# Streaming-encoder block: sums of x from its single-precision rows, norms tied to chunk numbers, another selection credit

## The chip, the cores and the metric

One core of a Trainium2 chip runs the whole kernel in one launch. The metric is device time in microseconds (us); the kernel before took 1354.08 us, the median of three executions (1351.22 to 1354.38). The hardware profiler recorded a further execution of 1351.62 us, and all rows below are from that one.

## The reference

One layer for 512 tokens of width 2048, in single precision:

```
h    = rmsnorm(x, norm_w);  proj = h @ w_in
a_q, a_f, a_i, a_g, c_q, c_kv, k_idx_raw, w_idx_raw, b_g, m_a, m_b = split(proj)
y_a  = gated linear recurrence(a_q, a_f, a_i) -> rmsnorm per head -> * silu(a_g)
cq   = rmsnorm(c_q);  q = cq @ w_uq;  q_idx = cq @ w_qidx          # 512 features
k, v = rmsnorm(c_kv) @ w_ukv;   k_idx = layernorm(k_idx_raw)
score = sum over 16 heads of relu(q_idx . k_idx) * w_idx           # per query and key
top 128 visible keys of each query -> attention over them with a relative bias = y_b
out  = rmsnorm(x + (sigmoid(m_a) * (y_a @ w_pa) + sigmoid(m_b) * (y_b @ w_pb)) @ w_out)
```

## The kernel before

**Products.** Every matrix product is made of three single-pass products of rounded high and low parts: `split` (L90) writes the high part on ScalarE and the low part (source less high part) on VectorE, and `mm3` (L94) issues the three matmuls. So every weight chunk is loaded by SyncE (`load`, L145, two raw buffers), split by ScalarE and VectorE (`prep`, L179, two chunks ahead), and only then used by TensorE.

**The start.** `start` (L289) loads x into tiles `x{t}` of pool `p0`, makes the row norms, transposes x on TensorE, and writes the scaled, transposed rows in single precision into tiles `y{t}{g}` (token block t, feature group g), also of `p0`. From these come the high and low parts `xh`, `xl`, which stay in place. The order of all this is the list `START_ORDER` (L20). The pool `p0` is then given up.

**Units with seven products.** The gate columns and the 512 columns of c_q are computed by `pair_unit` (L1227): a unit has eight chunks of 42 matmuls, and a 2x2 block scheme with seven products in place of eight. It needs four sums of blocks of x for each of eight row pairs k. `pair_early` makes them for seven of these: one VectorE addition of `xh` and `xl` (L1184) gives x back, `pair_sums_of` (L1174) makes four sums of 128x256, and `split` writes high and low parts into the tiles `s{k}` of pool `sums`. `pair_late` makes the eighth during the first unit. A unit ends with `evac` (L1255): one ScalarE copy (L1257) and seven VectorE instructions (L1258 to L1264) free its seven PSUM banks, for which the next unit's products wait; its stores go through ScalarE functions (L1268) and SyncE one and two pumps later, out of the tiles `c0` to `c3`.

**The pump.** After each chunk (or part of a job) `pump` (L224) issues loads, the stores that were put off, and then one step of the first generator of each lane (`hgrn`, `top`, `att`, `norm`, `misc`, `t5`, in this order). A generator gives way with `yield`; a step that has nothing to do is a bare `yield`. All engines take their instructions in the order in which they were issued here.

**Norms.** In the lane `norm`, during the gate units: `kidx_gen` (L618) normalises k_idx, `q_squares` (L542) sums the squares of c_q, which it loads from a scratch tensor into `c0` and `c1`, and `q_rows` (L576) loads c_q once more and scales and splits it. Their places are set by counts of bare `yield`s. Sums over the partitions are a matmul with ones (`row_sums`, L570); Ln and Exp on ScalarE (`rstd_row`, L536) make the root.

**Selection.** `top_gen` (L681) finds the 128 largest scores of each query, 48 rounds of `V.max` and `V.match_replace` (L695, L696) over 256, 384 and 512 keys. It runs beside the recurrence (`hgrn_gen`, L782), which sets `R.load` at each of its steps, and beside `norm_gen` (L592), the norm of c_kv. How many rounds a pump issues is set by a credit:

```
while credit <= 0:
    yield
    credit += 2.9 - R.load - bool(lanes["norm"])      # L692
credit -= 0.4 + 0.27 * (b + 1)                        # 0.94, 1.21, 1.48 for b = 1, 2, 3
```

**Behind the selection.** Job `uq_job(0)` leaves its two PSUM banks held (L1366); `open_att` (L1334) finishes the recurrence generators that are still due (gated output L963, L964, its split into `hy`, L969), then evacuates the two held banks (`uq_evac`, L983 on ScalarE and L984 on VectorE), and `ukv_job(0)` (L987) needs these banks for its second half.

Of the kernel before, what the change touches and what calls it, by code (L numbers as in the profile page):

```python
# [44 lines left out]
F32 = mybir.dt.float32  # L45
FR = mybir.dt.float32r
AF = mybir.ActivationFunctionType
OP = mybir.AluOpType
# [13 lines left out]
STILL, MOVED, RANK = 16, 48, 16  # L62

EVEN = 0
EARLY = 7
MO = (0, 128, 384, 768)


# [1 line left out]
def hybrid_block(ctx, tc, x, norm_w, w_in, lb_table, gnorm_a, q_norm_w, kv_norm_w, w_uq,  # L70
# [19 lines left out]
    def split(hi, lo, src):  # L90
        A.activation(hi, src, AF.Copy)  # L91
        V.tensor_tensor(lo, src, hi.bitcast(F32), op=OP.subtract)  # L92
# [37 lines left out]
    def enter(name, side=None, space=None):  # L130
        cm = tc.tile_pool(name=name, bufs=1, side=side, reuse_waits="tile")
        pools[name] = (cm, cm.__enter__())
        return pools[name][1]
# [1 line left out]
    def leave(name):  # L135
        pools.pop(name)[0].__exit__(None, None, None)

    R = SimpleNamespace(load=0.0)


    specs = []
# [146 lines left out]

    def start():  # L289
        R.v0 = enter("v0")  # L290
        p0 = enter("p0", side="right")
        ident = p0.tile([128, 128], F32, name="ident")
        A.dma_start(ident, c_ident)
        HF = D // 2
        nw = p0.tile([16, 128], F32, name="nw")
        wc = p0.tile([128, 16], F32, name="wc")
        xs = [[p0.tile([128, HF], F32, name=f"x{t}{i}") for i in range(2)] for t in range(4)]
        ys = [[p0.tile([128, 4, 128], F32, name=f"y{t}{g}") for g in range(4)] for t in range(4)]
        sq = p0.tile([128, HF], mybir.dt.bfloat16, name="sq")
        st = p0.tile([128, 4, 4], F32, name="st")  # L300
        rows = p0.tile([128, 128], F32, name="rows")
# [45 lines left out]
            return slice(t * 128, t * 128 + 128)  # L347

        def y_of(t, g):
            return ys[t][g]  # L350

        def factor(t, i):
            return st[:, t, i:i + 1]
# [58 lines left out]
                V.tensor_copy(widx[:, t, :], accs[t][:, 256:272])  # L412

        def dg(t):
            spreads[t] = diag, p0.tile([128, 128], F32, name=f"rrow{t}"), None
            V.tensor_scalar(spreads[t][0], ident, factor(t, 3), None, op0=OP.mult)

        def sp(t):
# [120 lines left out]
        A.activation(r, r, AF.Exp, scale=-0.5)  # L539
        return r  # L540

    def q_squares():  # L542
        for j0 in (0, 2):
            for _ in range(3):
                yield
            ts = [R.g.tile([128, 2, 256], F32, name=f"c{i}").rearrange("p a b -> p (a b)") for i in range(2)]
            for i, t in enumerate(ts):
                SP.dma_start(t, cq_d[j0 + i])
            yield
            yield  # L550
            for t in ts:
                A.activation(t, t, AF.Square)
            if j0 == 0:
                V.tensor_add(R.rq, *ts)
            else:
                V.tensor_add(ts[0], *ts)
                V.tensor_add(R.rq, R.rq, ts[0])
            for _ in range(3):
                yield
        sh, sl = R.cqh[:, 3, :], R.cql[:, 3, :]  # L560
        split(sh, sl, R.rq)
        yield
        ps = row_sums(sh, sl)
        for _ in range(2):
            yield
        rstd_row(ps, 512, R.rq)
        for _ in range(5):
            yield

    def row_sums(sh, sl):  # L570
        ps = bank("ns")
        mm(ps, ones_r, sh, True, False)
        mm(ps, ones_r, sl, False, True)
        return ps

    def q_rows():  # L576
        for j0 in (0, 2):
            for _ in range(3):
                yield
            ts = [R.g.tile([128, 2, 256], F32, name=f"c{i}").rearrange("p a b -> p (a b)") for i in range(2)]  # L580
            for i, t in enumerate(ts):
                SP.dma_start(t, cq_d[j0 + i])
            yield
            for i, t in enumerate(ts):
                V.scalar_tensor_tensor(t, t, c_qw[:, j0 + i:j0 + i + 1], R.rq, op0=OP.mult, op1=OP.mult)
                A.activation(R.cqh[:, j0 + i, :], t, AF.Copy)
                yield
                V.tensor_tensor(R.cql[:, j0 + i, :], t, R.cqh[:, j0 + i, :].bitcast(F32), op=OP.subtract)
            yield
            yield  # L590

    def norm_gen(raw, n, w, hi, lo):  # L592
        ss = []
# [16 lines left out]
        for j in range(n):  # L610
# [3 lines left out]
            yield  # L614
            V.tensor_tensor(lo[:, j, :], t, hi[:, j, :].bitcast(F32), op=OP.subtract)
            yield

    def kidx_gen():  # L618
        t, parts = R.rq, (R.cqh[:, 2, :], R.cql[:, 2, :])
        SP.dma_start(t, kx_d)  # L620
        for _ in range(3):
            yield
        split(*parts, t)
        yield
        ps = row_sums(*parts)
        for _ in range(2):
            yield
        V.scalar_tensor_tensor(t, ps, -1.0 / 128, t, op0=OP.mult, op1=OP.add)
        for _ in range(4):
            yield  # L630
        s = R.g.tile([128, 2, 256], F32, name="c3").rearrange("p a b -> p (a b)")
        A.activation(s, t, AF.Square)
        split(*parts, s)
        yield
        ps = row_sums(*parts)
        for _ in range(2):
            yield
        rstd_row(ps, 128, s)
        yield
        V.scalar_tensor_tensor(t, t, c_iw, s, op0=OP.mult, op1=OP.mult)  # L640
        V.tensor_scalar(t, t, c_ib, None, op0=OP.add)
        split(R.kih, R.kil, t)
        yield
        yield


    IDX_SCALE = 16 ** -0.5 * 128 ** -0.5

# [32 lines left out]
    def top_gen():  # L681

        credit = 0.0
        V.memset(R.M[:, 0:128], 0.0)
        for b in range(4):
            V.memset(R.M[0:64, MO[b] + b * 128 + 64:MO[b] + b * 128 + 128], NEG)
        for b in (1, 2, 3):
            m = R.M[:, MO[b]:MO[b] + b * 128 + 128]
            for i in range(16):
                while credit <= 0:  # L690
                    yield
                    credit += 2.9 - R.load - bool(lanes["norm"])  # L692
                credit -= 0.4 + 0.27 * (b + 1)
                m8 = R.s.tile([128, 8], F32, name="m8", bufs=2)
                V.max(m8, m)  # L695
                V.match_replace(m, m8, m, GONE)  # L696
                if i == 15:
                    V.tensor_scalar(m, m, -2e38, NEG, op0=OP.is_gt, op1=OP.mult)
# [438 lines left out]
    def open_norms():  # L1137
        R.c = enter("ranks", side="right")
        R.cqh = R.c.tile([128, 4, T], FR, name="cqh")
        R.cql = R.c.tile([128, 4, T], FR, name="cql")  # L1140
        R.r = enter("raws", side="right")
        R.kih = R.r.tile([128, T], FR, name="kih")
        R.kil = R.r.tile([128, T], FR, name="kil")
        R.rq = R.r.tile([128, T], F32, name="rq")
        R.i = enter("norms", side="right")
        R.x = enter("sums")

    def open_pairs():
        drain("norm")
# [18 lines left out]
            xs.append(cut + [a[:, 768:1024] if b is None else b])  # L1168
        return parts

    def pair_rows(k):
        return (x[k // 2][:, 2 * (k % 2):2 * (k % 2) + 2, :].bitcast(F32) for x in (xh, xl))

    def pair_sums_of(a, d):  # L1174
        a11, a21, a12, a22 = a
        V.tensor_tensor(d[0], a21, a22, op=OP.subtract)
        V.tensor_tensor(d[2], a11, a21, op=OP.subtract)
        V.tensor_tensor(d[1], d[0], a11, op=OP.subtract)
        V.tensor_tensor(d[3], d[1], a12, op=OP.add)

    def pair_early():
        for k in range(EARLY):
            a = R.i.tile([128, 2, T], F32, name="xa", bufs=2)
            V.tensor_tensor(a, *pair_rows(k), op=OP.add)  # L1184
            d = R.i.tile([128, 4, 256], F32, name="sv", bufs=2)
            pair_sums_of([a[:, i, j:j + 256] for i in (0, 1) for j in (0, 256)], [d[:, i, :] for i in range(4)])
            yield
            hi, hi4, lo, lo4 = sums_place(k)
            df = d.rearrange("p q n -> p (q n)")
            split(hi, lo, df[:, 0:768] if hi4 is not None else df)  # L1190
            if hi4 is not None:
                split(hi4, lo4, df[:, 768:])
            yield

    def pair_late():
        for k in range(EARLY, 8):
            ae, ao, da, db = (R.g.tile([128, 2, 256], F32, name=f"c{i}") for i in range(4))
            for i, a in enumerate((ae, ao)):
                V.tensor_tensor(a.rearrange("p a b -> p (a b)"), *(x[:, i, :] for x in pair_rows(k)), op=OP.add)
            pair_sums_of([a[:, j, :] for a in (ae, ao) for j in (0, 1)], [t[:, j, :] for t in (da, db) for j in (0, 1)])  # L1200
            yield
            hi, _, lo, _ = sums_place(k)
            for i, d in enumerate((da, db)):
                n = slice(i * 512, i * 512 + 512)
                split(hi[:, n], lo[:, n], d.rearrange("p a b -> p (a b)"))

    def x_pair(k):

# [18 lines left out]
    def pair_unit(at, n, rhs, evac, tokens_out=False, ahead={}):  # L1227
# [3 lines left out]
        for k in range(n):  # L1231
# [8 lines left out]
                    mm3(p[:, f, :], *ops, k == 0 and f == 0, k == n - 1)  # L1240
            if k == n - 1:
                evac(ps)
            pump()
            if k in ahead:
                ahead[k]()
# [49 lines left out]
    c_rhs = lambda k: (R.cqh[:, k, :], R.cql[:, k, :])  # L1295

    lane("misc", lb_gen)
    lane("misc", pair_early)
    feat_job(w_in, 4608, 2, NK, 4, x_rhs, ckv_evac)
    feat_job(w_in, 4864, 1, NK, 4, x_rhs, kx_evac)  # L1300
    ai_job(1, early=True)
    lane("misc", pair_late)
    pair_job(w_in, [4096, 4352], NK // 2, x_pair, pair_evac([cq_d[0:2], cq_d[2:4]], [None, None]))
    for gen in (kidx_gen, q_squares, q_rows):
        lane("norm", gen)
# [401 lines left out]
```

## Time and profile before

| | |
|---|---|
| median of three executions | 1354.08 us |
| profiled execution, whole | 1351.62 us |
| its span in the profile | 1349.8 us |
| TensorE matmul busy | 1327.1 us (98%) |
| TensorE weight load busy | 1244.6 us (92%) |
| VectorE busy | 1110.1 us (82%) |
| ScalarE busy | 698.7 us (52%) |
| GpSimd busy | 54.1 us (4%) |
| HBM read, written | 168.09 MB, 36.45 MB |

Busy time is the sum of an engine's instructions; what the span holds beyond it is idle time of that engine. The profiled execution is 1.8 us longer than its span: that is what lies around the program.

### The profile page before, as it was taken

The numbers are of one execution on the slowest core, as the hardware profiler recorded it, in microseconds if no ns is written. First come the engines' busy times: TensorE is split into PE (matmuls) and PEld (weight loads), VectorE is DVE, ScalarE is ACT, GpSimd is POOL, SyncE is SP. The second block draws the span as 40 slices with busy tenths as digits, with TensorE's granted clock in tenths as the row PEclk, the third lists the DMA queues.
The fourth block names the chain that finished last, engine by engine and source line by source line (L and its number), as shares of the span: only waits on it lengthen the run. The fifth ranks groups of instructions, "written<-read, shape, count | busy, mean of one in ns | idle before, by whom it ended". The sixth has DMA issues, their size and how long they took to land.

```text
span 1349.8 us, 27460 instructions
## 1 busy us (share of the span) xinstructions
PE 1327.1 (98%) x11202; PEld 1244.6 (92%) x11202; DVE 1110.1 (82%) x1805; ACT 698.7 (52%) x1129; POOL 54.1 (4%) x63
## 2 busy tenths in 40 slices
PE   8999999999999999999999999899999999999997
PEld 8889999999999999999999888788888888899996
DVE  7988888988889888886787989885656658899997
ACT  8444456555555444443765566546534334454454
POOL 0000000000000000000000000020101100001112
PEclk9999999999999999999999999999999999999999
DMA  6253444534544444444524324254856556654533
GB/s 225 58 167 113 149 138 128 161 122 141 172 146 152 141 141 141 115 136 143 191 70 142 111 80 126 90 171 153 287 164 204 199 172 218 209 181 144 201 141 126
DMA packets 143089, 204.76 MB, mean 152 GB/s; under 512 B 10689, under 2 KB 80882, under 8 KB 142834
## 3 DMA queue, kind: packets, MB, share of 16 engines
q1 hardware_dynamic: 142674, 202.74, 47.4%
q8 instruction: 88, 1.44, 0.4%
q14 instruction: 39, 0.32, 0.1%
q10 hardware_dynamic: 288, 0.26, 0.1%
HBM read 168.09 MB, written 36.45 MB: 152 GB/s over the span
## 4 chain that ended last, share of the span: by engine, by line
PE 91%; DVE 5%; ACT 2%; DMA 1%; issue 1%; SPq 0%; DVEq 0%; ACTq 0%
PE pp L95 16%; PE pp L97 16%; PE pp L96 16%; PE acc L95 11%; PE acc L97 11%; PE acc L96 11%; PE hl L100 1%; PE ho L100 1%; PE acc L100 1%; DVE xl L390 1%; PE sc L95 1%; PE sc L96 1%; PE sc L97 1%; DMA fr<-in_w_in_dram 0%; DVE wl L92 0%
## 5 line engine op out<-in xcount | busy, mean ns | idle before, releaser
L174 ACT ACTIVATE wh<-sv 128x512 fp32r<-128x512 f32 x280 | 169.2, 626 | 132.8 <-DVE sv L167 90.4
L172 ACT ACTIVATE bh<-wr 128x768 fp32r<-128x768 f32 x140 | 118.2, 844 | 183.7 <-PE pp L96 75.5
L95 PE MATMUL pp<-s,wh 128*128 128x256 f32 x672 | 185.8, 276 | 1.9 <-DVE c L1262 1.9
L96 PE MATMUL pp<-s,wh 128*128 128x256 f32 x672 | 185.5, 276 | 0.0
L97 PE MATMUL pp<-s,wl 128*128 128x256 f32 x672 | 185.5, 276 | 0.0
L176 DVE TENSOR_TENSOR wl<-sv,wh 128x1024 fp32r<-128x1024 f32 x140 | 171.0, 1221 | 4.9
L175 DVE TENSOR_TENSOR bl<-wr,bh 128x768 fp32r<-128x768 f32 x140 | 133.6, 954 | 43.8 <-ACT bh L172 43.8
L95 PEld LDWEIGHTS pp<-s,wh 128*128 128x128 f32 x672 | 126.1, 188 | 2.2 <-issue 2.2
L97 PEld LDWEIGHTS pp<-s,wl 128*128 128x128 f32 x672 | 126.2, 188 | 0.0
L96 PEld LDWEIGHTS pp<-s,wh 128*128 128x128 f32 x672 | 126.2, 188 | 0.0
L95 PE MATMUL pp<-xh,bh 128*128 128x256 f32 x448 | 123.8, 276 | 0.7 <-ACT c L1257 0.7
L97 PE MATMUL pp<-xh,bl 128*128 128x256 f32 x448 | 123.7, 276 | 0.0
L96 PE MATMUL pp<-xl,bh 128*128 128x256 f32 x448 | 123.7, 276 | 0.0
L167 DVE TENSOR_TENSOR sv<-wr 128x512 f32<-128x512 f32 x140 | 98.2, 702 | 4.2 <-DMA wr<-in_w_in_dram 2.5
L95 PE MATMUL acc<-yh,wh 128*128 128x512 f32 x256 | 100.2, 391 | 0.0
L92 DVE TENSOR_TENSOR wl<-wr,wh 128x1024 fp32r<-128x1024 f32 (+1 forms) x66 | 79.4, 1202 | 25.1 <-ACT wh L91 24.9
L97 PE MATMUL acc<-yh,wl 128*128 128x512 f32 x256 | 99.8, 390 | 0.0
L96 PE MATMUL acc<-yl,wh 128*128 128x512 f32 x256 | 99.7, 390 | 0.0
L91 ACT ACTIVATE wh<-wr 128x1024 fp32r<-128x1024 f32 (+1 forms) x66 | 68.1, 1032 | 61.1 <-PE acc L96 36.2
L95 PE MATMUL acc<-xh,wh 128*128 128x512 f32 x240 | 96.2, 401 | 0.0
L97 PE MATMUL acc<-xh,wl 128*128 128x512 f32 x240 | 93.9, 391 | 1.2 <-DVE wl L92 1.2
L96 PE MATMUL acc<-xl,wh 128*128 128x512 f32 x240 | 93.5, 390 | 0.0
(405 smaller groups left out, 3799.4 us busy)
## 6 DMA issues: line engine op xcount, KB each, us to landing
wr<-in_w_in_dram SPq DMA_DIRECT2D x136, 512.0 KB, 3.7
wr<-in_w_out_dram SPq DMA_DIRECT2D x28, 512.0 KB, 3.8
mg<-gate_d SPq DMA_DIRECT2D x48, 256.0 KB, 3.5
gate_d<-c SPq DMA_DIRECT2D x44, 256.0 KB, 4.9
wr<-in_w_in_dram SPq DMA_DIRECT2D x36, 256.0 KB, 2.9
wr<-in_w_pa_dram SPq DMA_DIRECT2D x16, 512.0 KB, 4.0
wr<-in_w_pb_dram SPq DMA_DIRECT2D x16, 512.0 KB, 4.1
wr<-in_w_qidx_dram SPq DMA_DIRECT2D x8, 512.0 KB, 3.3
```

Of the source, the lines that this page charges most:

```text
L91: A.activation(hi, src, AF.Copy)
L92: V.tensor_tensor(lo, src, hi.bitcast(F32), op=OP.subtract)
L95: PE.matmul(ps, lh, rh, start=first, stop=False, skip_group_check=True)
L96: PE.matmul(ps, lh, rl, start=False, stop=False, skip_group_check=True)
L97: PE.matmul(ps, ll, rh, start=False, stop=last, skip_group_check=True)
L100: PE.matmul(ps, l, r, start=first, stop=last, skip_group_check=True)
L167: V.tensor_tensor(sv[:, 0:2, :], b[:, 1:3, :], b[:, 0:1, :].to_broadcast([128, 2, 256]), op=OP.add)
L172: A.activation(bh, b[:, 1:4, :], AF.Copy)
L174: A.activation(vh[:, i:i + 2, :], sv[:, i:i + 2, :], AF.Copy)
L175: V.tensor_tensor(bl, b[:, 1:4, :], bh.bitcast(F32), op=OP.subtract)
L176: V.tensor_tensor(vl, sv, vh.bitcast(F32), op=OP.subtract)
L390: V.tensor_tensor(xl[g][:, :, tokens(t)], y_of(t, g), xh[g][:, :, tokens(t)].bitcast(F32), op=OP.subtract)
```

## The change

Three things. First, x and y are tiles of the pool `sums` and stay: y is one tile per feature group, `[128, 2048]`, and `pair_gen` makes the sums straight from it, two row pairs at a time (four instructions of 128x512 each), for all eight; `pair_early`, `pair_late` and the addition of `xh` and `xl` go. The sums of the first four row pairs are written over the tiles of x, those of the last four over the tiles of y. Second, the norm generators wait for chunk numbers (`chunk(2)`: go on in a pump after chunk 2 of a unit); `q_squares` loads c_q once, into the places of `cqh`, and `q_rows` reads it there. Third, the credit of the selection loses 0.3 in place of 1 while the lane `norm` is not empty.

```diff
-EARLY = 7
-    R = SimpleNamespace(load=0.0)
+    R = SimpleNamespace(load=0.0, chunk=0)
 def start():
+        R.x = enter("sums")
-        nw = p0.tile([16, 128], F32, name="nw")
+        nw = p0.tile([128, 128], F32, name="nw")[0:16, :]
-        xs = [[p0.tile([128, HF], F32, name=f"x{t}{i}") for i in range(2)] for t in range(4)]
-        ys = [[p0.tile([128, 4, 128], F32, name=f"y{t}{g}") for g in range(4)] for t in range(4)]
+        xs = [R.x.tile([128, 2048 + 64 * (t == EVEN)], F32, name=f"x{t}", tag=f"s{t}") for t in range(4)]
+        xs = [[x[:, 0:HF], x[:, HF:D]] for x in xs]
+        R.ys = [R.x.tile([128, 2048], F32, name=f"y{g}", tag=f"s{4 + g}").rearrange(
+            "p (t j n) -> p t j n", t=4, j=4) for g in range(4)]
...
+    def chunk(*ks):
+        yield
+        while R.chunk not in ks:
+            yield
+    def spare(i):
+        return R.g.tile([128, 2, 256], F32, name=f"c{i}").rearrange("p a b -> p (a b)")
+    def q_squares():
+        raw = [R.cqh[:, j, :].bitcast(F32) for j in range(4)]
+        for j in range(4):
+            SP.dma_start(raw[j], cq_d[j])
+        for j in (0, 2):
+            yield from chunk(2 + j // 2)
+            s = [spare(j), spare(j + 1)]
+            for i in range(2):
+                A.activation(s[i], raw[j + i], AF.Square)
...
+        yield from chunk(0)
+        split(R.cql[:, 0, :], R.cql[:, 1, :], R.rq)
+        yield
+        ps = row_sums(R.cql[:, 0, :], R.cql[:, 1, :])
+        for _ in range(2):
+            yield
+        rstd_row(ps, 512, R.rq)
+    def kidx_gen():
...
+        yield from chunk(2)
+        split(*parts, t)
+        yield
+        ps = row_sums(*parts)
+        yield
+        yield from chunk(0)
+        V.scalar_tensor_tensor(t, ps, -1.0 / 128, t, op0=OP.mult, op1=OP.add)
+        yield from chunk(2)
+        s = spare(3)
+        A.activation(s, t, AF.Square)
+        split(*parts, s)
+        yield
+        ps = row_sums(*parts)
+        yield
+        yield from chunk(0)
+        A.activation(ps, ps, AF.Ln, bias=eps, scale=1.0 / 128)
+        A.activation(ps, ps, AF.Exp, scale=-0.5)
+        yield from chunk(1)
+        V.scalar_tensor_tensor(t, t, c_iw, ps, op0=OP.mult, op1=OP.mult)
+        V.tensor_scalar(t, t, c_ib, None, op0=OP.add)
+        yield from chunk(2)
+        split(R.kih, R.kil, t)
+        yield
     def q_rows():
...
+        for j in range(4):
+            yield from chunk(2)
+            t = spare(0)
+            V.scalar_tensor_tensor(t, R.cqh[:, j, :].bitcast(F32), c_qw[:, j:j + 1], R.rq, op0=OP.mult, op1=OP.mult)
+            A.activation(R.cqh[:, j, :], t, AF.Copy)
+            yield from chunk(3)
+            V.tensor_tensor(R.cql[:, j, :], t, R.cqh[:, j, :].bitcast(F32), op=OP.subtract)
+        yield
 def top_gen():
-                    credit += 2.9 - R.load - bool(lanes["norm"])
+                    credit += 2.9 - R.load - 0.3 * bool(lanes["norm"])
-    def pair_early():
...
-    def pair_late():
...
+    def pair_gen():
+        for g, y in enumerate(R.ys):
+            d = R.i.tile([128, 2, 4, 256], F32, name="sv", bufs=2)
+            a11, a21, a12, a22 = (y[:, t:t + 2].rearrange("p t (k i) n -> p t k i n", i=2)[:, :, :, i, :]
+                                  for i in (0, 1) for t in (0, 2))
+            q = [d[:, :, i, :].rearrange("p k (t n) -> p t k n", t=2) for i in range(4)]
+            V.tensor_tensor(q[0], a21, a22, op=OP.subtract)
+            V.tensor_tensor(q[2], a11, a21, op=OP.subtract)
+            V.tensor_tensor(q[1], q[0], a11, op=OP.subtract)
+            V.tensor_tensor(q[3], q[1], a12, op=OP.add)
+            yield
+            for i in range(2):
+                hi, hi4, lo, lo4 = sums_place(2 * g + i)
+                df = d[:, i].rearrange("p q n -> p (q n)")
+                split(hi, lo, df[:, 0:768] if hi4 is not None else df)
+                if hi4 is not None:
+                    split(hi4, lo4, df[:, 768:])
+                yield
 def pair_unit(...):
+            R.chunk = k
             pump()
-    lane("misc", pair_early)
+    lane("misc", pair_gen)
-    lane("misc", pair_late)
```

## Rows read from the trace of the kernel before

**Rows 1.** The page: the span, and busy time, share of the span and instructions of each engine.

```profile
span 1349.8 us, 27460 instructions
PE 1327.1 (98%) x11202; PEld 1244.6 (92%) x11202; DVE 1110.1 (82%) x1805; ACT 698.7 (52%) x1129; POOL 54.1 (4%) x63
```

**Rows 2.** What TensorE waited for in the whole span: the waiting line, the releaser, us in total, times, the longest.

```profile
PE acc L95 <- DVE aq L984: 5.4, 1, 5.4
PE pp L95 <- DVE c L1262: 1.9, 2, 1.1
PE pt L377 <- DMA x<-in_x_dram: 1.6, 1, 1.6
...
PE acc L97 <- DVE wl L92: 1.2, 1, 1.2
PE acc L96 <- DVE wl L92: 0.9, 1, 0.9
...
PE pp L95 <- ACT c L1257: 0.7, 1, 0.7
```

**Rows 3.** The timeline of TensorE, only matmuls ahead of which it was idle (start, duration, instruction, idle time and what ended it).

```profile
70.63 0.50 PE L97 MATMUL acc<-xh,wl 128*128 128x512 f32 x1 [1.21 <-DVE wl L92]
...
77.24 0.39 PE L96 MATMUL acc<-wl,xh 128*128 128x256 f32 x1 [0.88 <-DVE wl L92]
...
215.36 0.39 PE L95 MATMUL pp<-xh,bh 128*128 128x256 f32 x1 [0.70 <-ACT c L1257]
...
219.63 0.36 PE L95 MATMUL pp<-s,wh 128*128 128x256 f32 x1 [1.11 <-DVE c L1262]
...
411.75 0.36 PE L95 MATMUL pp<-s,wh 128*128 128x256 f32 x1 [0.76 <-DVE c L1262]
...
877.65 0.58 PE L95 MATMUL acc<-wh,ckh 128*128 128x256 f32 x1 [5.41 <-DVE aq L984]
```

**Rows 4.** VectorE's groups of instructions between 50 and 112 us, by line and shape: count, busy us and mean ns of one, idle time before them.

```profile
L1184 DVE TENSOR_TENSOR xa<-xh,xl 128x1024 f32<-128x1024 f32 x7 | 8.5, 1219 | 0.0
...
L167 DVE TENSOR_TENSOR sv<-wr 128x512 f32<-128x512 f32 x5 | 3.4, 685 | 0.0
L1179 DVE TENSOR_TENSOR sv<-sv,xa 128x256 f32<-128x256 f32 x7 | 3.0, 425 | 0.2
```

**Rows 5.** The timeline of VectorE around the two waits at 70 and 77 us, and then one row of ScalarE.

```profile
67.16 1.22 DVE L1184 TENSOR_TENSOR xa<-xh,xl 128x1024 f32<-128x1024 f32 x1
...
69.89 0.68 DVE L92 TENSOR_TENSOR wl<-wr,wh 128x512 fp32r<-128x512 f32 x1
...
75.96 1.23 DVE L92 TENSOR_TENSOR wl<-wr,wh 128x1024 fp32r<-128x1024 f32 x1 [0.31 <-ACT wh L91]
...
74.87 1.06 ACT L91 ACTIVATE wh<-wr 128x1024 fp32r<-128x1024 f32 x1 [3.28 <-DMA wr<-in_w_in_dram]
```

**Rows 6.** The timeline of VectorE, and then of ScalarE, in the gate units between 180 and 220 us.

```profile
209.98 0.74 DVE L640 SCALAR_TENSOR_TENSOR rq<-rq,cols,c 128x512 f32<-128x512 f32 x1
...
211.94 0.69 DVE L92 TENSOR_TENSOR kil<-rq,kih 128x512 fp32r<-128x512 f32 x1 [0.70 <-ACT kih L91]
...
216.08 0.68 DVE L1258 TENSOR_TENSOR c<-pp,c 128x512 f32<-128x512 f32 x1
...
218.80 0.68 DVE L1262 TENSOR_TENSOR c<-pp,c 128x512 f32<-128x512 f32 x1
...
181.75 2.19 ACT L1268 ACTIVATE c<-c 128x512 f32<-128x512 f32 x4
...
191.81 0.63 ACT L632 ACTIVATE c<-rq 128x512 f32<-128x512 f32 x1 [2.63 <-DMA gate_d<-c]
...
205.09 1.28 ACT L539 ACT_TABLE_LOAD   x1
...
214.73 0.58 ACT L1257 ACTIVATE c<-pp 128x512 f32<-128x512 f32 x1
```

**Rows 7.** The timeline of VectorE from 869 us on: the last two rounds of the selection, and what follows them.

```profile
869.38 0.69 DVE L695 MAX8 m<-M 128x8 f32<-128x512 f32 x1
...
870.89 0.69 DVE L695 MAX8 m<-M 128x8 f32<-128x512 f32 x1
...
872.75 0.74 DVE L963 SCALAR_TENSOR_TENSOR hk<-ho,cols,hk 128x512 f32<-128x512 f32 x1
...
875.52 1.47 DVE L92 TENSOR_TENSOR hy<-hk,hy 128x512 fp32r<-128x512 f32 x2
876.91 1.28 DVE L984 SCALAR_TENSOR_TENSOR aq<-acc,aq 128x512 fp32r<-128x512 f32 x2
```

**Rows 8.** The timeline of ScalarE in the same stretch: the last of the four instructions that `L963` needs.

```profile
868.91 1.06 ACT L958 ACTIVATE hk<-hk 128x1024 f32<-128x1024 f32 x1
```

**Rows 9.** Two stretches of 5 us: start:end, length, then busy us and instructions of PE, PEld, DVE, ACT and POOL, the granted TensorE clock, DMA share and GB/s; below them the matmul with which the next job begins.

```profile
875.00:880.00 5.00, 2.35 (x11) 2.35 (x12) 4.88 (x8) 3.63 (x6) 0.00 (x0) 0.52 0.57 211
880.00:885.00 5.00, 5.00 (x26) 4.59 (x26) 2.98 (x5) 2.14 (x3) 0.00 (x0) 0.80 0.86 289
...
882.52 0.40 PE L95 MATMUL acc<-xh,wh 128*128 128x512 f32 x1
```

**Rows 10.** The timeline of VectorE in the recurrence beside which rounds are moved: the first instruction after a score product, and the first half of a round over 256 keys.

```profile
721.11 0.69 DVE L834 TENSOR_TENSOR hq<-hq,tot 128x512 f32<-128x512 f32 x1 [0.74 <-PE hl L100]
...
730.26 0.42 DVE L695 MAX8 m<-M 128x8 f32<-128x256 f32 x1
```

More of the change, by code (lines that the diff above doesn't have):

```diff
@@ L349, in y_of @@
         def y_of(t, g):
-            return ys[t][g]
+            return R.ys[g][:, t]
         def factor(t, i):
@@ L414, in dg @@
         def dg(t):
-            spreads[t] = diag, p0.tile([128, 128], F32, name=f"rrow{t}"), None
+            spreads[t] = diag, p0.tile([128, 128], F32, name=f"rrow{t}", tag=("rrow", "nw")[t]), None
             V.tensor_scalar(spreads[t][0], ident, factor(t, 3), None, op0=OP.mult)
@@ L540, in rstd_row @@
         return r
[L542 to L548, printed above, removed]
-            yield
[L550 to L568, printed above, removed]
+    def chunk(*ks):
+        yield
+        while R.chunk not in ks:
+            yield
+    def spare(i):
+        return R.g.tile([128, 2, 256], F32, name=f"c{i}").rearrange("p a b -> p (a b)")
     def row_sums(sh, sl):
@@ L574, in row_sums @@
         return ps
-    def q_rows():
[L577 to L590, printed above, removed]
+    def q_squares():
[7 more added lines that the diff above has]
+                A.activation(s[i], raw[j + i], AF.Square)
+            if j == 0:
+                V.tensor_add(R.rq, *s)
+            else:
+                V.tensor_add(s[0], *s)
+                V.tensor_add(R.rq, R.rq, s[0])
+        yield from chunk(0)
[5 more added lines that the diff above has]
+        rstd_row(ps, 512, R.rq)
@@ new lines, in kidx_gen @@
+    def kidx_gen():
+        t, parts = R.rq, (R.cqh[:, 2, :], R.cql[:, 2, :])
+        SP.dma_start(t, kx_d)
+        yield
[22 more added lines that the diff above has]
+        yield
@@ L616, in norm_gen @@
             yield
[L618 to L644, printed above, removed]
     IDX_SCALE = 16 ** -0.5 * 128 ** -0.5
@@ L1145, in open_norms @@
         R.i = enter("norms", side="right")
-        R.x = enter("sums")
     def open_pairs():
@@ L1169, in sums_place @@
         return parts
[L1171 to L1179, printed above, removed]
-    def pair_early():
[L1182 to L1186, printed above, removed]
-            yield
[L1188 to L1193, printed above, removed]
@@ L1195, in pair_late @@
-    def pair_late():
[L1196 to L1205, printed above, removed]
+    def pair_gen():
[8 more added lines that the diff above has]
+            V.tensor_tensor(q[3], q[1], a12, op=OP.add)
+            yield
+            for i in range(2):
[5 more added lines that the diff above has]
+                yield
```

## The prediction

> **What bounds the kernel now.** I read the page's busy times first: TensorE's matmuls fill 1327.1 of 1349.8 us [rows 1], so everything that is not TensorE idle time or a lower TensorE clock can give back nothing, and VectorE's 82% matter only where TensorE waits for it. The change takes no matmul away. So the most that it can bring is in the list of TensorE's waits [rows 2], and the second view, TensorE's timeline, says where they lie [rows 3]: two early ones on low parts of weights (70.63 and 77.24 us: 1.21 + 0.88 = 2.09), three at the head of a unit, on its predecessor's evacuation (215.36, 219.63, 411.75: 0.70 + 1.11 + 0.76 = 2.57), and one of 5.41 ahead of 877.65, on the evacuation of the held banks behind the selection. These three places are just those that the three parts of the change touch. Third, the table of stretches: after the long wait the granted clock is 0.52 of full speed in 875 to 880 us and 0.80 in 880 to 885 [rows 9], that is, TensorE works at its lower level (1.2 GHz) for a while. Before that it had stood still for those 5.41 us. With 2.35 us of work in the first stretch and 5 in the second this cost about 2.35 x 0.48 + 5 x 0.20 = 2.1 us.
>
> **Part A, sums of x.** It removes seven additions of 1.22 us, and 28 instructions of 0.42 become part of 16 of 128x512, each some 0.69 by another instruction of that shape [rows 4]: 20 us of VectorE for seven row pairs become 11 for eight. The splits stay. The eighth pair's work leaves the first unit, where TensorE did not wait for it: worth nothing there. At 70 us VectorE is behind TensorE: it had just added x [rows 5], and the low part that TensorE wanted at 70.63 - 1.21 = 69.4 came at 69.89 + 0.68 = 70.6. Up to there the lane had made four sums and three splits, 4 x 2.9 = 11.6 us without the splits. The new one is at its third step of sums, 3 x 4 x 0.69 = 8.3, and at one more split, about 1.2: 2.1 us less, more than the 1.2 that are missing. The second wait hangs on a load that ScalarE waited for [rows 5]; SyncE can issue it when the first low part has freed the raw buffer, so it too comes about 2 us sooner, and the low part ends near 75.1, with TensorE wanting it near 75.2: covered, but barely. Bounds 1.2 (the load does not follow) to 2.09; I take **2.0**.
>
> What is late next: the same loads. What is added: four-dimensional operands on the sums; I price them as plain ones, and the cover at this place is VectorE's new slack. The shared tiles (x in one tile per token block, y in one per feature group) cost something only if a transpose were to wait for the other half of x, one more wait like the 1.61 us on x [rows 2]; I take 0, since `xh` was such a shared tile already and was written and read by regions. Bounds 0 and 1.6.
>
> **Part B, norms by chunk.** Ahead of 215.36 the end of `kidx_gen` ran in the last chunks of a unit: two table loads of 1.28 us each, the last products at 209.98, the split at 211.94 [rows 6]. So ScalarE's evacuation copy came at 214.73, VectorE's share of it began at 216.08 and reached L1262, for which TensorE waited, at 218.80 [rows 6]. In the new order nothing of a norm is left for chunks 4 to 7, and the lateness must be made up by then. I take the 411.75 wait, on the same line, for the same thing with `q_rows`. Moved with the steps: Ln and Exp of `kidx_gen` now queue on ScalarE in the first pump of a unit behind the 2.19 us of stores [rows 6], with about 4 us of their own; the split of the coming chunk waits behind them, VectorE behind that, and TensorE has two prepared chunks as cover. `spare(0)` makes VectorE wait, in four units, for a store to land, as ScalarE did for 2.63 us in the unit before 215 [rows 6]; TensorE waited for nothing behind that until 215.36 [rows 3], so I price these at 0, with the lost cover as a lateness of 2.6 us at chunk 2 that five chunks have to absorb. The c_q loads on SyncE's queue fall from eight to four, issued in one pump, in front of a weight load that lies two chunks ahead: 0. The three waits are worth 2.57 if all go and 0 if new lateness takes their place; one leftover of half a microsecond in a crowded unit (squares, or Ln and Exp) seems fair: **2.1**.
>
> **Part C, the credit.** By the code the lane `norm` is full for eight additions to the credit, so 8 x 0.7 = 5.6 more is credited, 3.8 rounds at the last price of 1.48. I followed the credit pump by pump with the loads that the recurrence sets: the last round is issued two pumps earlier, and the last two pumps, which had two rounds each, have none. The rounds are 870.89 - 869.38 = 1.51 us apart, and the gated output L963 stood behind them until 872.75 [rows 7]. The other thing that L963 needs, the Exp, ended at 868.91 + 1.06 = 869.97 [rows 8]. So of 6 us of rounds taken away only 872.75 - 870.03 = **2.72** reach TensorE: the next lateness is ScalarE's Ln and Exp, bound to TensorE's own products, then L963, L964, `hy` and the evacuation, the same chain of 877.65 - 872.75 = 4.9 us as before [rows 3, 7]. The wait shrinks from 5.41 to 2.69 and does not go. Bounds 0 to 5.41.
>
> Then the clock. A pause of 1.61 us [rows 2] was followed by nothing of the kind, one of 5.41 by the lower level. 2.69 lies between, nearer to the first; I take the full clock, **2.1** more, with ends 0 and 2.1.
>
> The rounds moved forward lie beside the recurrence. The worst new neighbour is ahead of 721.11: two more rounds over 256 keys, about 0.9 each by the half round of 0.42, against an idle time of 0.74 [rows 10]; one us of lateness runs into the next step, whose score product I see losing **0.1**. Bounds 0 and 1.1.
>
> **Sum.** 2.0 + 2.1 + 2.72 + 2.1 - 0.1 = 8.8 us. Against the profiled execution that gives 1351.62 - 8.8 = 1342.8. The executions known lie in two pairs, 1351.22 and 1351.62, 1354.08 and 1354.38; the profiled one is 2.5 below the median shown. I take the middle of the four, 1352.85, and forecast **1344.0**.
>
> **The rivals.** *The clock falls all the same.* The new pause of 2.69 us is longer than any that this trace shows without a fall, so the granted clock may read as in 875 to 885 once more [rows 9]: 2.1 us are not won, 1346.1. The Trainium skill, TensorE: Matmul & The Clock Gate, section on the HAM clock gate, speaks for it: the monitor's window runs freely, so one and the same pause can cost the clock in one execution and not in the next; this trace has one fall only and cannot show that. Chance 0.12.
>
> *The early parts do not do what they say.* The low parts at 70 and 77 us wait for loads rather than for VectorE, and the heads of units find other lateness (VectorE behind a store). For it: the ScalarE row that waits 3.28 us for a load [rows 5] and the 2.63 [rows 6]; against it: the releasers named are VectorE's [rows 2]. Only part C is left, 4.8 us: 1348.0. Chance 0.12.
>
> *Slower: the moved rounds hold up the recurrence.* VectorE takes its work in order; a round that sits between a score product and the next decay holds the following score product. By my count five pumps get an extra round there. It decides where a round exceeds VectorE's idle time, 0.74 at 721.11 [rows 10]. At up to 1.51 each that is 7.5 us, and the gated output is then as late as it was, so part C gives nothing: 1352.85 - 4.1 + 7.5 = 1356.3. Against it: rounds that come earlier are also rounds that are missing later, so VectorE catches up. Chance 0.06.
>
> *Nothing shows*: all is given back in small waits, 1351 to 1354. Chance 0.05. The forecast itself has 0.65.
>
> **How the numbers follow.** The low end is the fastest time shown less everything, 1351.22 - (2.09 + 2.57 + 5.41 + 2.1) = 1339; the high end takes in the rival with part C alone and two us of scatter. Range 1339.5 to 1350. A measurement of this kernel tells about 0.3% (4 us) from no change, so faster means below 1350. That holds nearly all of the forecast (0.63 of 0.65), most of the clock's rival (0.10) and under half of the third (0.05): 0.78. Slower (above 1358) is part of the recurrence's rival and of what I have not thought of: 0.06. The rest, 0.16, is the same.
>
> **What would show it.** Right: no wait on a low part near 70 to 77 us; none at the heads of the units at 215 and 411; a wait on L984 of 2 to 3.5 us with the granted clock at 1.00 behind it; L963 straight behind the Exp, not behind a round. Wrong: that wait at 5 us again, or none at all (then I have mistaken what L963 waits for); a clock under 0.9 after it; waits of score products on VectorE between 700 and 860 us; an evacuation that begins late in the units with squares or with Ln and Exp; a start longer by over a microsecond.

## The result and the profile after

The changed kernel takes 1345.38 us (median of four executions, 1344.59 to 1346.9) against 1353.26 for the kernel before on the same chip: a ratio of 0.9945, 95% interval 0.9928 to 0.9962. Five further executions in another session gave 1346.65 against 1352.32, a ratio of 0.9957 (0.9945 to 0.997); the median of all nine is 1345.67. The forecast of 1344.0 was 1.4 to 1.7 us too low. The profiled execution took 1345.36 us with a span of 1343.5. All rows below come from it unless another kernel is named. Of all executions behind this document one, of the kernel of experiment 11, took 2699.77 us, about twice the others; no profile shows why, and its ratio leaves it out.

First the page: the span and TensorE's busy time, which fell by 1.0 only [rows 1].

```profile
span 1343.5 us, 27423 instructions
PE 1326.1 (99%) x11202; PEld 1243.8 (93%) x11202; DVE 1095.7 (82%) x1779; ACT 700.7 (52%) x1128; POOL 53.7 (4%) x63
```

What TensorE waited for (line, releaser, us in total, times, longest); it answers to [rows 2]. L981 is the line that was L984, L1242 that was L1262, L91 that was L92.

```profile
PE acc L94 <- DVE aq L981: 2.7, 1, 2.7
PE pp L94 <- DVE c L1242: 1.9, 2, 1.0
...
PE acc L95 <- DVE wl L91: 0.7, 1, 0.7
PE acc L96 <- issue: 0.7, 1, 0.7
```

TensorE's timeline, matmuls with idle time ahead, answering to [rows 3]. The first wait on a low part is gone and the second remains; the heads at 215 and 219 us are clean, but one at 293 is new and the one at 411 (now 409) stays; the long wait is halved; and at 881 there is a gap for which the profile names no releaser.

```profile
75.39 0.39 PE L95 MATMUL acc<-wl,xh 128*128 128x256 f32 x1 [0.74 <-DVE wl L91]
...
292.91 0.36 PE L94 MATMUL pp<-s,wh 128*128 128x256 f32 x1 [1.03 <-DVE c L1242]
...
408.91 0.36 PE L94 MATMUL pp<-s,wh 128*128 128x256 f32 x1 [0.87 <-DVE c L1242]
...
872.31 0.39 PE L94 MATMUL acc<-wh,ckh 128*128 128x256 f32 x1 [2.67 <-DVE aq L981]
...
881.43 0.50 PE L96 MATMUL acc<-xh,wl 128*128 128x512 f32 x1 [0.66 <-issue]
```

The stretches of 5 us behind the long wait [rows 9]: here the granted clock (the column of 1.00) did not fall.

```profile
870.00:875.00 5.00, 2.69 (x22) 2.70 (x23) 4.88 (x8) 4.23 (x7) 0.00 (x0) 1.00 0.56 210
875.00:880.00 5.00, 5.00 (x147) 4.13 (x146) 4.79 (x7) 2.26 (x3) 0.17 (x1) 1.00 0.86 288
```

**Where the time went, by stages.** The arrival of x moves everything by up to 1.3 us from one execution to the next (the first matmul of the c_kv columns starts at 40.86 to 42.12 us in these profiles). So I count from that matmul and cut the span at five events that all kernels have: ScalarE's first evacuation copy (stage S, part A), the last (G, the gate units, part B), the first product of the job behind the selection (R, the rounds), the first product of the gate job (P, the pause with the clock), and the product at 940 that waits 0.6 us on `gs` in every kernel (L). From there to the end all need 403.3 us (the kernel of experiment 5 needs 403.8). The number in brackets is that of the experiment below; "kernel 2" is the kernel of experiment 2.

| kernel | S | G | R | P | L | sum |
|---|---|---|---|---|---|---|
| before | 92.31 | 500.40 | 235.16 | 13.17 | 64.00 | 905.04 |
| changed | 90.33 | 499.44 | 235.37 | 8.54 | 64.95 | 898.63 |
| changed, second profile (4) | 90.99 | 500.01 | 235.09 | 9.96 | 64.08 | 900.13 |
| before, new credit (1) | 92.19 | 501.11 | 236.18 | 10.02 | 64.03 | 903.53 |
| changed, old credit (2) | 91.23 | 500.00 | 235.37 | 13.02 | 64.02 | 903.64 |
| the latter, pause filled (3) | 90.23 | 499.22 | 235.45 | 11.28 | 64.03 | 900.21 |
| changed, pause filled (5) | 90.15 | 500.21 | 235.06 | 8.55 | 64.02 | 897.99 |
| changed, scratch elsewhere (6) | 91.03 | 497.74 | 235.02 | 9.65 | 64.38 | 897.82 |
| changed, scratch order (7) | 90.99 | 497.04 | 235.63 | 10.03 | 64.00 | 897.69 |
| changed, bare step (8) | 90.13 | 499.78 | 235.07 | 10.05 | 64.00 | 899.03 |
| changed, banks (9) | 90.27 | 500.41 | 235.67 | 5.60 | 65.98 | 897.93 |
| three edits together (10) | 90.14 | 496.94 | 235.00 | 5.60 | 65.93 | 893.61 |
| the same, v later (11) | 90.12 | 497.62 | 235.51 | 5.60 | 64.74 | 893.59 |

So in the changed kernel's first profile S fell by 1.98, G by 0.96 only, P by 4.63, and L rose by 0.95, of which 0.66 is the gap at 881. No run has the sums of x or the norms alone: S holds the first and G the second, and by these stages the two are told apart.

### The profile page after: what moved, and what is told of

The parts are those of the page before. It is cut to its first block, busy times and chain, and to the rows that moved or that the text cites. A ratio compares the mean times of both kernels' runs of the same rounds, so it can differ in the third digit from the quotient of the medians.

```text
span 1343.5 us, 27423 instructions
## 1 busy us (share of the span) xinstructions
PE 1326.1 (99%) x11202; PEld 1243.8 (93%) x11202; DVE 1095.7 (82%) x1779; ACT 700.7 (52%) x1128; POOL 53.7 (4%) x63
## 4 chain that ended last, share of the span: by engine, by line
PE 92%; DVE 4%; ACT 2%; DMA 1%; issue 1%; SPq 0%; DVEq 0%; ACTq 0%
PE pp L94 16%; PE pp L95 16%; PE pp L96 16%; PE acc L94 12%; PE acc L96 11%; PE acc L95 11%; PE hl L99 1%; PE ho L99 1%; PE acc L99 1%; DVE xl L392 1%; PE sc L94 1%; PE sc L95 1%; PE sc L96 1%; DMA wr<-in_w_in_dram 1%; DMA fr<-in_w_in_dram 0%
## 5 line engine op out<-in xcount | busy, mean ns | idle before, releaser
L91 DVE TENSOR_TENSOR wl<-wr,wh 128x1024 fp32r<-128x1024 f32 (+1 forms) x66 | 78.6, 1191 | 28.3 <-ACT wh L90 28.3
```

## The experiments

Times are medians against the kernel before of the same session (1352.62, 1352.35 and 1352.32 us in the three, each on another chip). Of these three the changed kernel itself ran in the third only, and the intervals of its two ratios overlap those of kernels 5 to 9. So a difference of 1 or 2 us to it is shown by the stages and rows, not by the times alone.

**1. The credit alone**, in the kernel before.

```diff
-                    credit += 2.9 - R.load - bool(lanes["norm"])
+                    credit += 2.9 - R.load - 0.3 * bool(lanes["norm"])
```

> The kernel before with the third part of the change alone (the credit loses 0.3 in place of 1 while the lane norm is not empty). My theory: the selection's last rounds no longer stand in front of the gated output, so the pause of 5.41 us shrinks to about 2.7 and the clock stays at 1.00 behind it: 4.6 to 4.9 us under the kernel before, and the waits at 70, 77, 215, 219 and 411 us stay as they were. Rival (the credit is worth only the pause, the clock falls whatever its length): 2.7 us. Rival (the moved rounds hold the recurrence up): under 2 us, with new waits of score products between 700 and 860 us.

1349.11 us, 3.5 under the kernel before (ratio 0.9973, 0.9962 to 0.9983): between my theory and the first rival. The pause is 2.67, but the clock behind it is not full:

```profile
875.00:880.00 5.00, 3.97 (x20) 3.97 (x21) 4.60 (x7) 3.25 (x6) 0.00 (x0) 0.66 0.61 191
```

That costs 3.97 x 0.34 = 1.35 us. P is 10.02, 1.5 more than in the changed kernel's first profile, with the same pause. The second rival falls: R is 1.0 longer, but 0.75 of that is one gap at 722 us that waits for nothing, and no score product waits on VectorE. The waits at 70, 77, 215, 219 and 411 us stayed, as expected.

**2. The old credit back**, in the changed kernel (the edit of 1 reversed).

> The changed kernel with the old credit (1 in place of 0.3): the first two parts alone. My theory: the pause of about 5.4 us and the lower clock behind it come back, 4.6 to 4.9 us over the changed kernel and some 2.9 under the kernel before (1.9 from the sums of x, 1.0 from the norms), with the waits of 1.03 and 0.87 us at the heads of two units still there. Rival (the earlier sums and norms move the pause as well): under 3 us over the changed kernel.

1349.72 us, 2.9 under the kernel before (ratio 0.998, 0.9971 to 0.9988) and 4.1 over the nine executions of the changed kernel. The pause is 5.41 and the clock 0.89, 0.50 and 0.93 in the three stretches from 870 to 885 us; the middle one:

```profile
875.00:880.00 5.00, 3.29 (x15) 3.29 (x16) 4.58 (x7) 3.66 (x7) 0.00 (x0) 0.50 0.62 210
```

The parts add: 3.5 + 2.9 = 6.4, against 6.9 for all (1352.62 to 1345.67 us).

**3. The pause of the old credit filled.**

```diff
+            if p == 0:
+                warm = bank("warm")
+                for _ in range(20):
+                    mm(warm, wh[:, 0, 0:128], R.ckh[:, 0, :], True, True)
```

> The kernel of the old credit, with 20 extra products of 128x512 (work that the reference does not need, into a bank that nobody reads) issued to TensorE just ahead of the product that waits. They need nothing of the late evacuation, so they run inside the pause. My theory that the pause costs twice, once as a wait and once through the clock: the pause stays a loss of about 5.4 us, the granted clock stays at 1.00 behind it, and the time is about 2.1 us under the kernel with the old credit. Rival (the low clock behind the pause costs nothing since the work there waits for loads or for ScalarE anyway): no change, within 0.5 us, although the clock is at 1.00. Rival (the fill runs past the end of the pause): slower by what is left over, up to 4 us.

1348.43 us, 1.3 under kernel 2; P falls from 13.02 to 11.28, by 1.74. The remaining idle time is 0.9 and the clock never leaves 1.00:

```profile
870.00:875.00 5.00, 4.11 (x22) 3.22 (x21) 4.83 (x8) 3.30 (x6) 0.00 (x0) 1.00 0.43 160
875.00:880.00 5.00, 5.00 (x36) 4.24 (x36) 4.78 (x7) 3.12 (x5) 0.00 (x0) 1.00 0.73 248
```

So the clock is a cost of its own, 1.7 of my 2.1; work that nobody needs won it back.

**4. The changed kernel again**, not edited.

> The changed kernel itself, not edited. Its profile above shows the full clock behind the pause of 2.67 us, while four other kernels with the same pause of 2.67 show 0.66 to 0.72 in one stretch of 5 us there, and it shows an idle stretch of 0.66 us at 881 that waits for nothing, which those do not have. My theory (both are properties of one execution): this profile shows a granted clock of 0.65 to 0.75 in a stretch behind the pause, no idle stretch of 0.66 us at 881, and the median is 1345 to 1346. Rival (both belong to the kernel): clock 1.00 and the same idle stretch.

1346.65 us. The pause is 2.67 once more, the gap at 881 is not there, and the clock fell:

```profile
870.00:875.00 5.00, 2.33 (x15) 1.80 (x14) 4.84 (x8) 3.65 (x6) 0.00 (x0) 0.99 0.51 191
875.00:880.00 5.00, 5.00 (x24) 4.71 (x24) 3.33 (x6) 2.76 (x5) 0.00 (x0) 0.67 0.71 239
```

One and the same program kept its clock in one execution and lost 1.4 us to it in another (P 8.54 and 9.96). The theory holds for both rows; the median was 0.65 over its range.

**5. The pause of 2.67 filled**, the edit of 3 with 10 products, in the changed kernel.

> The changed kernel, with 10 extra products of 128x512 (0.23 us each at the full clock, work that the reference does not need, into a bank that nobody reads) in the pause of 2.67 us. My theory (in most executions the clock falls behind the pause and costs 1.2 to 1.5 us): the pause is left at about 0.4 us, the clock is 1.00 behind it, and the time is 0.9 to 1.4 us under the changed kernel run beside it. Rival (the changed kernel mostly keeps its clock, as its first profile shows): within 0.4 us.

1344.45 us, 2.2 under kernel 4 in the same session (ratios to before 0.9942, 0.9929 to 0.9956, and 0.9957, 0.9945 to 0.997, which overlap: the sign is not shown by the times alone). The stages show it: P is 8.55 with an idle time of 0.4 and the clock at 1.00, 1.41 under kernel 4. That 8.55 equals the first profile's 8.54 fits a first profile that had simply kept its clock.

**6. Scratch of the norms elsewhere.**

```diff
-            s = [spare(j), spare(j + 1)]
+            s = [R.cql[:, j + i, :] for i in range(2)]
...
-            t = spare(0)
+            t = R.cql[:, j, :].bitcast(F32)
```

> The changed kernel, with the scratch rows of the norms written over parts of the low rows of c_q in place of the tiles c0 to c3, out of which the stores of the unit before still go. What it changes in the output: the squares and the scaled rows of c_q are rounded to the type of the products. My theory (ScalarE and VectorE stand behind a store in the units of squares and of scaled rows, and that lateness reaches the evacuation): the waits of 1.03 us at 293 and 0.87 us at 409 go, 1.5 to 2.0 us under the changed kernel. Rival (these units are too full, whatever the stores do): the waits stay, within 0.4 us.

1344.49 us, 1.2 under the nine executions of the changed kernel; G falls to 497.74. Both waits are gone; another, 0.61, shows at the head at 254.67. The time gained is less than the 1.5 to 2.0 expected.

**7. The same scratch tiles in another order.**

```diff
-            s = [spare(j), spare(j + 1)]
+            s = [spare(1 - j // 2), spare(3 - j // 2)]
...
-            t = spare(0)
+            t = spare(1)
```

> The changed kernel, with the same scratch tiles in another order: the squares and the scaled rows take first the tiles whose stores are issued first. My theory (behind a store): the wait at 409 us goes and that at 293 us falls to about 0.35, 1.2 to 1.6 us under the changed kernel. Rival (too full): both stay, within 0.4 us.

1344.01 us (ratio 0.9936, 0.9924 to 0.9949), 1.7 under the changed kernel; G is 497.04, 2.4 to 3.0 under it, and no head of a unit waits. How the stores did it is in the rows of ScalarE and VectorE. The changed kernel, ScalarE at the first square and then VectorE in the two units (269.62 and 385.93):

```profile
268.43 1.15 ACT L566 ACTIVATE c<-cqh 128x512 f32<-128x512 f32 x2 [2.99 <-DMA gate_d<-c]
```

```profile
269.62 0.69 DVE L568 TENSOR_TENSOR rq<-c,c 128x512 f32<-128x512 f32 x1 [2.85 <-ACT c L566]
...
385.93 0.75 DVE L612 SCALAR_TENSOR_TENSOR c<-cqh,cols,rq 128x512 f32<-128x512 f32 x1 [1.62 <-DMA qf_d<-c]
```

With the other order, the same instructions:

```profile
268.04 0.63 ACT L566 ACTIVATE c<-cqh 128x512 f32<-128x512 f32 x1 [1.32 <-DMA gate_d<-c]
268.99 0.63 ACT L566 ACTIVATE c<-cqh 128x512 f32<-128x512 f32 x1 [0.32 <-DMA gate_d<-c]
```

```profile
383.73 0.75 DVE L612 SCALAR_TENSOR_TENSOR c<-cqh,cols,rq 128x512 f32<-128x512 f32 x1
```

Each step behind a store still waits, but for a store that was issued earlier: 2.99 becomes 1.32 + 0.32, and 1.62 becomes too little to be listed. Kernels 6 and 7 take away the same wait by different means and clear the same two heads; the rival (units too full) falls. G parts them without overlap: 499.22 to 500.41 in the seven profiles that keep the scratch of the change, 496.94 to 497.74 in the four that do not (kernels 6, 7, 10 and 11).

**8. A bare step ahead of the third step of sums.**

```diff
         for g, y in enumerate(R.ys):
+            if g == 2:
+                yield
```

> The changed kernel, with one bare step of the generator ahead of its third step of sums, so that this step no longer stands in front of the low part that TensorE waits for at 75 us. My theory (VectorE still holds up the raw buffer, and with it the load): the wait of 0.74 us goes, 0.6 to 0.9 us under the changed kernel, and the sums end one pump later with no new wait. Rival (the load is late by itself, on SyncE's queue): no change at 75 us. Rival (the sums of the last rows come too late for the first unit): a new wait between 90 and 130 us, no gain.

1345.31 us: 0.4 under the changed kernel, which the times cannot tell from nothing. In the trace the wait is gone. A low part now stands ahead of the sums that begin at 65.47, so the raw buffer came free at 65.5 and not at 68.7, and the low part that TensorE waited for begins at 72.00 and not at 74.11. Counted from the first matmul of the c_kv columns, which lies 0.64 earlier in this execution, that is 2.5 and 1.5 us sooner (VectorE):

```profile
64.86 0.68 DVE L91 TENSOR_TENSOR wl<-wr,wh 128x512 fp32r<-128x512 f32 x1
65.47 0.69 DVE L1175 TENSOR_TENSOR sv<-y 128x512 f32<-128x512 f32 x1
...
72.00 1.23 DVE L91 TENSOR_TENSOR wl<-wr,wh 128x1024 fp32r<-128x1024 f32 x1 [1.56 <-ACT wh L90]
```

So VectorE's place was the cause and not SyncE's queue; S is 90.13, 0.2 and 0.9 under the two profiles of the changed kernel. Nothing new waits; what of the 0.74 did not come back is in the pace of the matmuls (last section).

**9. Banks of its own** for the second half of the first ukv job.

```diff
-                ps = mmp.tile([128, T], F32, name="acc")
+                ps = bank("uv") if p == 0 else mmp.tile([128, T], F32, name="acc")
```

> The changed kernel, with the second half of the first ukv job in two banks of its own, so that it no longer waits for the evacuation of the held banks. My theory: the remaining wait of 2.7 us was for those banks alone; it goes, and the time falls by 2.2 to 2.7 us. Rival (the next product is late as well, since the outputs behind the evacuation are made on the same engines): the wait goes to the next job's products, under 1 us gained. Rival (the banks are still in use by the recurrence): a new wait of about the same size, no change.

1344.13 us (ratio 0.994, 0.9926 to 0.9954), 1.5 under the changed kernel. The pause and the clock's fall are gone (P 5.60), 2.9 and 4.4 under its two profiles, and 1.9 to 2.0 come back as a new wait of a score product:

```profile
PE hl L99 <- DVE hqs L820: 1.6, 1, 1.6
```

So neither text was whole: the wait was for those banks, and VectorE is what is late next; that its own order of work makes it late is for experiment 11.

**10. Kernels 7, 8 and 9 together.**

> The changed kernel with three edits together: the second half of the first ukv job in banks of its own, the other order of the scratch tiles, and the bare step ahead of the third step of sums. By itself the first gave 1.2 us by the medians, with a new wait of 1.6 us of a score product on VectorE behind it. My theory: the gains add, 1.2 + 1.4 + 0.7 = 3.3 us, about 1342.0. Rival (early gains are lost at the selection, whose rounds are late by as much): 1.2 us, as with the banks alone, 1344.

1340.76 us, a ratio of 0.9913 (0.9899 to 0.9926): 4.9 under the changed kernel, more than the 3.3 of my sum, whose 1.2 for the banks was the smallest of the estimates. TensorE's list of waits has one row over 0.7 behind the start:

```profile
PE hl L99 <- DVE hqs L820: 1.7, 1, 1.7
PE acc L336 <- POOL ones_r L306: 1.4, 1, 1.4
PE acc L99 <- ACT fh L395: 1.3, 1, 1.3
PE acc L94 <- ACT gs L1267: 0.6, 1, 0.6
```

**11. In kernel 10, v split behind the next step of the recurrence.**

```diff
-                split(*(a[:, t2 * 2:t2 * 2 + 2, :] for a in v), ps.rearrange("p (t n) -> p t n", t=2))
+                vs.append(([a[:, t2 * 2:t2 * 2 + 2, :] for a in v], ps.rearrange("p (t n) -> p t n", t=2)))
+                if p:
+                    split(*vs[t2][0], vs[t2][1])
             lanes["att"].append(att_gen(p))
             pump()
+            for out, ps in vs if p == 0 else ():
+                split(*out, ps)
```

> The kernel with the three edits together, and the split of the first v behind the next step of the recurrence on ScalarE and VectorE. There the score product waits 1.67 us on VectorE, which had just done the low parts of v (1.28 us). My theory (VectorE is the bound of this stretch, by its order): the wait falls to about 0.4 and the time by 1.0 to 1.3 us, 1339.5. Rival (VectorE is full for 15 us, so what is put off is late at the next place): under 0.5 us, with a new wait of attention products.

1340.46 us, a ratio of 0.9909 (0.9896 to 0.9923). The wait fell and nothing took its place; L is 64.74 against 65.93:

```profile
PE hl L99 <- DVE hqs L820: 0.5, 1, 0.5
```

That confirms the mechanism in the trace (VectorE's order of work), but the times do not tell the two kernels apart: G was 0.7 longer in this execution and a gap of 0.6 without a releaser fell into R. Either version beats both the kernel before and the changed one.

## Why the prediction was right, and where it was wrong

**Part A, sums of x: right in size, one step wrong.** "Covered, but barely" failed by 0.74. In this profile the third step of sums still stands ahead of the low part that frees the raw buffer (VectorE):

```profile
67.42 0.69 DVE L1176 TENSOR_TENSOR sv<-sv,y 128x512 f32<-128x512 f32 x1
68.02 0.69 DVE L91 TENSOR_TENSOR wl<-wr,wh 128x512 fp32r<-128x512 f32 x1
...
74.11 1.23 DVE L91 TENSOR_TENSOR wl<-wr,wh 128x1024 fp32r<-128x1024 f32 x1 [1.91 <-ACT wh L90]
```

The low part came 1.87 us sooner than its 69.89 [rows 5], and the next one 1.85, ending at 75.34 and not at 75.1. TensorE wanted it at 75.39 - 0.74 = 74.65 and not near 75.2, since the first wait had cost it more than the 1.21 of idle time (last section). Kernel 8 moved that step and the wait went. By idle time A would have won 1.21 + 0.88 - 0.74 = 1.35. By the stage it is 1.98; of the other seven profiles that keep the wait, three show 2.0 to 2.2 and four 1.1 to 1.3, the four at the slower pace of matmuls told of in the last section. The 2.0 of the forecast is thus met where the pace is that of the kernel before.

**Part B, norms by chunk: the term that was mis-sized.** 2.1 was forecast; G fell by 0.96, 0.39 and 0.40 in the first, second and old-credit profiles, and by -0.01 to 1.18 in the four others that keep this part as it is. Their mean is 499.87 against 500.40 and 501.11 in the two profiles with the old norms: a gain of some 0.9. The step that failed is "so I price these at 0, with the lost cover as a lateness of 2.6 us at chunk 2 that five chunks have to absorb": they did not. VectorE has no idle time to catch up in: behind 385.93 it pauses for less than 0.1 us at a time until its evacuation at 405. Two of the three waits named went, one stayed and a new one of 1.03 took back more than half of what the two gave. Kernel 7 shows the size: without the waits behind stores G falls by 3.4 against the kernel before, more than my 2.57.

**Part C: the pause right, the clock wrong in most executions.** 5.41 - 2.72 = 2.69 was forecast and 2.67 is in every profile with the new credit whose pause was left alone, and `L960` stands straight behind the Exp as I said (VectorE):

```profile
858.40 0.69 DVE L692 MAX8 m<-M 128x8 f32<-128x512 f32 x1
...
867.39 0.75 DVE L960 SCALAR_TENSOR_TENSOR hk<-ho,cols,hk 128x512 f32<-128x512 f32 x1 [2.99 <-ACT hk L955]
```

The first row is the last round of the selection, which began at 870.89 [rows 7]; in kernel 1, with the credit alone, it begins at 862.13. From `L960` to the product that waits it is 872.31 - 867.39 = 4.92, the 4.9 of the forecast.

The first profile gave the full clock, as forecast, and would by itself have confirmed "nearer to the first; I take the full clock". The other five profiles with a pause of 2.67 (kernels 1, 4, 6, 7 and 8) lost it: 0.66 to 0.72 in a stretch of 5 us, and P longer by 1.1 to 1.5. Kernels 6, 7 and 8:

```profile
870.00:875.00 5.00, 4.34 (x25) 4.34 (x26) 4.23 (x7) 2.90 (x6) 0.00 (x0) 0.72 0.68 224
```

```profile
870.00:875.00 5.00, 3.66 (x18) 3.66 (x19) 4.60 (x7) 3.57 (x6) 0.00 (x0) 0.66 0.59 195
```

```profile
870.00:875.00 5.00, 3.49 (x16) 3.49 (x17) 4.38 (x7) 3.67 (x7) 0.00 (x0) 0.66 0.64 205
```

So the rival that I gave 0.12 is the usual case, at a lower price than its 2.1. The Trainium skill, TensorE: Matmul & The Clock Gate, section on the HAM clock gate, says that the monitor's window runs freely: the two profiles of one program agree with it, but no run here shows that this is the reason. The typical gain in P is 3.2, not 4.82.

**Moved rounds: right.** R is 235.00 to 235.67 with the new credit (one of 236.18 holds a gap of 0.75) and 235.16 to 235.45 with the old. The slower rival is refuted: no score product waits on VectorE between 700 and 860 us.

**The sum.** By the stages part A brought 1.1 to 2.2, part B some 0.9 and part C 3.2 in most executions, so 5.2 to 6.3, against 8.8 forecast; the medians give 6.9 (1352.62 to 1345.67). The first profile, 6.4 by the stages, had the luck of its clock less 0.95 in L. So the forecast gain was too large by about 2 us, mostly in part B and the clock. The forecast time came closer, within 1.4 to 1.7 us, because its base was 1352.85 and not the profiled 1351.62, which took 1.2 off the miss.

## What to carry to other kernels

When a step is moved to an idle place, ask which transfer still holds the buffer that it writes: the order in which scratch tiles were taken was worth 2.4 to 3.0 us of its stage here, as much as the move itself was meant to bring. Count a TensorE pause twice, as a wait and as a chance of a lower clock, and don't read that chance from one profile. Compare two traces by the time between events that both have: start-up scatter and gaps without a releaser are then seen for what they are.

## What the runs showed of the hardware

**The clock by length of pause**, in 13 profiles: after 5.41 it fell in two of two, after 2.67 in five of six, after 1.64 and 1.67 (the new wait of kernels 9 and 10) in none, after 0.9, 0.5 and 0.4 (kernels 3, 11 and 5) in none. The pauses of kernels 9 to 11 lie ahead of another product, so the length is not all that differs.

**Gaps without a releaser.** Four profiles have TensorE gaps of 0.4 to 0.75 us put down to "issue", at 717 to 722 or at 881 us, and the second profile of the changed kernel has none: in this kernel they belong to an execution. Their cause stays open.

**Two paces of the same matmuls.** Between 90 and 96 us, with the clock at 1.00 and no idle time, matmuls of 128x256 follow each other every 0.113 us in one execution and every 0.118 in another; one execution can show both, as the changed kernel's first profile does with 0.118 between 97 and 101 us. One stretch of the changed kernel, and then the same one of kernel 7 (count of PE instructions in brackets):

```profile
90.00:96.00 6.00, 6.00 (x55) 6.00 (x54) 4.27 (x7) 1.15 (x2) 0.00 (x0) 1.00 0.47 160
```

```profile
90.00:96.00 6.00, 6.00 (x53) 6.00 (x52) 3.89 (x6) 1.16 (x2) 0.00 (x0) 1.00 0.53 170
```

The weight load is busy throughout (the second figure, 6.00). The whole job of such products, from its first one to the unit behind it, took 22.80 us in the changed kernel's first profile (74.37 to 97.17) and 23.61 in its second (74.87 to 98.48). That is 0.8 us for one and the same program. Among the profiles that keep the wait at 75 us, S is 91.0 to 91.2 in the four at the slower pace and 90.2 to 90.3 in the four at the faster; kernel 8, without that wait but at the slower pace, shows 90.13. What sets the pace was not tried.

**Idle time understates a stall.** Ahead of 70.63 [rows 3] the previous matmul started at 69.03 in the same timeline, 1.60 earlier where 0.23 is the pace; so 1.37 were lost and not the 1.21 shown, since a matmul's end is put later than the next can start:

```profile
69.03 0.39 PE L96 MATMUL acc<-xl,wh 128*128 128x512 f32 x1
70.63 0.50 PE L97 MATMUL acc<-xh,wl 128*128 128x512 f32 x1 [1.21 <-DVE wl L92]
```

Matmul by matmul, the first profile of the changed kernel differs from it by more than 0.03 us at four places of stage S only: it saves 1.38 here and 0.11 right behind, 0.23 just ahead of the second wait and 0.24 in it. That is 1.96 of the 1.98 by which S fell.
